# Turning q, k and v in two parts, with the loads behind the store, in a decoder layer on one core

## The chip, the cores and the metric

The kernel runs on one core of a Trainium2 chip. Its time is the device time of one execution in microseconds, the median of the runs shown. A core has TensorE (PE, matrix products, with its weight loads shown apart as PEld), VectorE (DVE), ScalarE (ACT), GpSimd (POOL) and SyncE (SP); here SP and POOL issue nearly all DMA transfers. SBUF is the memory on the chip that all operands pass through, PSUM holds the results of PE.

## The reference

One layer of a decoder on 512 new tokens and, beside them, on 8 single tokens with a state of their own (520 columns in all):

```python
xn = rmsnorm(h, norm_mix)
proj = xn @ w_in                         # q | k | v | z | beta, decay logits | pool channels
qkv_c, new_conv = short_conv(conv_buf, qkv, conv_w)      # 4 taps along time, then silu
q = l2norm(q) * 128 ** -0.5;  k = l2norm(k)
o, S = gated_delta_chunked(q, k, v, g, beta, S0)         # 8 heads of 128, chunks
dn_out = rmsnorm(o, dn_norm) * silu(z)
pool_out = multiscale_pool(p) ...
h = h + concatenate([dn_out, pool_out]) @ w_out
gu = rmsnorm(h, norm_ffn) @ w_gate_up
h = h + (silu(gu[:, :5632]) * gu[:, 5632:]) @ w_down

# gated_delta_chunked, per head and chunk
kb = k * beta
m = strict_lower((kb @ k.T) * decay)
u = triangular_solve(I + m, v * beta)
w = triangular_solve(I + m, kb * exp(g))
qk = lower((q @ k.T) * decay)
v_new = u - w @ S                        # chunk after chunk
o = (q * exp(g)) @ S + qk @ v_new
S = S * exp(g_last) + (k * exp(g_last - g)).T @ v_new
```

The model has a width of 2048; the state of the 512 tokens starts at zero, and so do the three rows ahead of the convolution (its left edge).

## The kernel before

**Products.** All data are fp32, cut into a high and a low part; each product of a tile of 128 weight columns is three matmuls (high·high, high·low, low·high, L168 to L170) for each of 16 blocks of the depth and for each of two chunks of columns (264 and 256). That is 96 matmuls, written out by `product()`, the second chunk three blocks behind the first. The results go to three PSUM banks (`mm`), from which DVE evicts them (`normed_out`, L259). Weights come as `raw` by SP (L131), ACT makes `hi` (L135), DVE makes `lo` (L137).

**What is woven in.** PE executes in the order in which the program writes its instructions. Between the products, `product()` calls `weave.step()` once per block of depth, six matmuls. A `Weave` holds tracks of generators: at each step, the first generator of each track goes on to its next `yield`, and the number that it yields is the number of steps to its next turn; `add(task, track, delay)` puts a task at the end of a track, to start no sooner than `delay` steps from now. A step is thus a distance on PE. The other engines have their instructions ordered by the framework's scheduler, by priority and by when operands are there, and each engine and each DMA queue works its list in order.

**The mixer.** For two batches `b` of four heads `h` (0 to 3, then 4 to 7) the program runs:
- four key tiles: product, convolution over 3 + 512 columns in a tile `ext` whose left three columns are zero (`columns()`, L263; the taps at L739), silu (L740), a turn of the blocks, and 16 steps later `keys(h)`, which makes the Gram matrix of k, its sums of squares (L799 to L808), the masked matrix of each chunk into `mixb` (L810) and stores its diagonal blocks of 32 (`nd_d`, L816);
- `eliminate(b)`: loads the blocks of four heads (`nb`, L825), clears `u` (L829), inverts all blocks in 62 steps on DVE (L835, L837), copies the transpose (`ut`, L840), and stores both (`ud_d`, L838, L841);
- four z tiles (called z0 to z3 below for b = 0);
- for each head `qv_tiles(h)`: loads the inverted blocks (`utf`, L1117), the v tile, the q tile, and then `delta(h)`. The products for v and q of this head stand on PE around the delta of the head before.

`delta(h)` begins with `decay(h)` (broadcast `gcb` by SP, four subtractions on DVE to `dm`, L779, an exponential on ACT, L781), the exponential of `gcb` (L851) and q's scaling `qts` (L853). Then comes what is called the solution here: four matmuls `nn`·`utf` to `xp` (L859), their copy `xt_` on ACT (L861), a copy of `utf` to `cur` on POOL (L863), and three times (`it`) four matmuls of `xt_` (L869) with the combination of their result on DVE (L871), at a distance of two steps. After the last, q·k and its decay (`aq`, L881). The decay of the keys (`kd`, L874) and the scaling of v (L754) are put on DVE between them. Then four chunks in turn, with the state `S` (L909) handed on.

**A turn.** k, q, v and the result are needed with time along the partitions too. `turn_blocks` does this with one transpose of 32 x 32 blocks on DVE (L766, L763), a store to memory (`tok_d`, L768) and four loads back (L771), all five transfers issued by POOL one after the other. Each load waits on POOL's queue for the store to be through.

Of the kernel before, what the change touches and what calls it, by code (L numbers as in the profile page):

```python
# [8 lines left out]
F32 = mybir.dt.float32  # L9
# [3 lines left out]
ALU = mybir.AluOpType  # L13
# [29 lines left out]
class Weave:  # L43
# [3 lines left out]
    def __init__(self):  # L47
        self.tracks, self.wait, self.now = ([], []), [0, 0], 0
# [21 lines left out]
def decoder_kernel(ctx, tc, x_prompt, x_sample, state_delta, state_conv, state_pool, norm_mix, w_in,  # L70
# [189 lines left out]

    def columns():
        ext = pre.tile([P, 3 + SEQ], F32, tag="ext", name="ext", bufs=2)
        pool.memset(ext[:, 0:3], 0.0)  # L263
        return ext
# [256 lines left out]
    with ExitStack() as p1:  # L521
# [235 lines left out]
        def turn_blocks(kind, h, src, dst):  # L757
# [7 lines left out]
            else:  # L765
# [3 lines left out]
                rows = d.rearrange("(i p) (j f) -> j p i f", p=32, j=4)  # L769
            for j in range(4):  # L770
                pool.dma_start(dst[32 * j:32 * j + 32, :].rearrange("p (n q) -> p n q", n=rows.shape[2]), rows[j])  # L771

# [17 lines left out]
        def keys(h):  # L790
# [26 lines left out]
            for q in range(4):  # L817
                r = slice(32 * q, 32 * q + 32)
                pool.memset(nn3[r, :, r], 0.0)


        def eliminate(b):
# [5 lines left out]
            yield 10  # L828
# [16 lines left out]
        def delta(h, qT, qk, vs):  # L845
# [6 lines left out]
            qts = d1tile("qts", [P, SEQ], "qts")  # L852
            dve.tensor_tensor(qts, qT, gcb, op=ALU.mult)  # L853
# [11 lines left out]
            for it in range(3):  # L865
# [9 lines left out]
                if it == 2:  # L875
# [4 lines left out]
                    for c in range(NCH):  # L880
                        dve.scalar_tensor_tensor(aq[:, ck(c)], gq_[:, ck(c)], fk[:, c:c + 1], dm[:, ck(c)],  # L881
                                                 op0=ALU.mult, op1=ALU.mult)
                if it == 1:
                    scaled(vs, ik)
# [4 lines left out]
            for c in range(NCH):  # L889
# [26 lines left out]
                if c == 1:  # L916
                    ss = d1tile("ss", [P, NCH], "ss")
                    junk = d1tile("junk", [P, P], "junk")
                    for j in range(NCH):
                        act.activation(by_column(junk), by_chunk(qk)[:, j], AF.Square, accum_out=ss[:, j:j + 1])  # L920
# [16 lines left out]
            turn_blocks(3, h, on, on)  # L937
            weave.add(gate(h, on), 1, 12)
# [174 lines left out]
        def qv_tiles(h):  # L1113
# [6 lines left out]
            turn_blocks(2, h, vs, vs)  # L1120
            qT = d1tile("s0", [P, SEQ], "qT")
            qkv_tile(0, h, qT)
            qk = d1tile("tq", [P, SEQ], "qk")
            turn_blocks(0, h, qT, qk)
            weave.add(delta(h, qT, qk, vs), 0, 1)

        kds = {}
        for b in range(2):
            for h in range(4 * b, 4 * b + 4):
# [5 lines left out]
                kds[h] = d1tile("kd", [P, SEQ], "kd")  # L1135
                turn_blocks(1, h, mixb[:, h % 4, 0:SEQ], kds[h])
# [23 lines left out]
        for t in (6, 7, 4, 5, 2, 3, 0, 1):  # L1160
            pool_tile(t, operands)
            if t % 2:
                weave.add(pool_mix(t // 2, *splits[t // 2]), 1, 12 if t > 1 else 7)
# [942 lines left out]
```

## Time and profile before

| | |
|---|---|
| median of 3 runs | 2160.54 us (2160.06 to 2163.25) |
| profiled execution | 2161.12 us |
| its span | 2159.4 us |
| PE, PEld busy | 2127.0 us (98%), 2118.4 us (98%) |
| DVE, ACT, POOL busy | 1772.2 us (82%), 919.9 us (43%), 531.4 us (25%) |
| mean granted clock of PE | 0.998 |
| moved by DMA | 313.84 MB, 145 GB/s on the mean |

The span is the time from the first to the last instruction on the core; 1.7 us of the execution lie around it. Busy times of one engine do not add to those of another, since the engines work side by side. A row of the timeline shows start, duration, engine, line, operation, output and inputs, shape, and in brackets the idle time of that engine just before it and what ended it. A row of the waits shows the engine, its output and line, the engine, tile and line that it waited for, and then the sum of the waits, their number and the longest.

### The profile page before, as it was taken

The page shows a single profiled execution, that of the slowest core. Times are in us where ns is not written, and L with a number is a line of the kernel's source. Part 1 is how long each engine was busy: PE and PEld are TensorE (multiplying, and loading weights), DVE is VectorE, ACT ScalarE, POOL GpSimd, SP SyncE. Part 2 cuts the span into 40 slices and gives each one's busy share as a digit, 9 for nine tenths or more (in the row PEclk, how much of TensorE's full clock was granted, in tenths as well). Part 3 has the DMA queues.
Part 4 walks back from the last instruction along what each step waited for, and adds up shares of the span by engine and source line. Part 5 has one row for each costly group of instructions (what it writes and reads, how often), then busy time and mean ns, then how long its engine had stood idle before and what let it go on. Part 6 is the DMA issues. An engine that isn't in the chain of part 4 may idle for free.

```text
span 2159.4 us, 43083 instructions
## 1 busy us (share of the span) xinstructions
PE 2127.0 (98%) x17681; PEld 2118.4 (98%) x17681; DVE 1772.2 (82%) x2715; ACT 919.9 (43%) x1340; POOL 531.4 (25%) x672
## 2 busy tenths in 40 slices
PE   8999999999999999999999999999999999999998
PEld 7999999999999999999999999999999999999998
DVE  7886677667599979988988988988877898887997
ACT  6433433343264544434434434434334444435444
POOL 2413441332012202233233233232113302003100
PEclk9999999999999999999999999999999999999999
DMA  8444454544445533554554454454456746438333
GB/s 281 126 125 118 130 141 122 132 125 126 122 118 162 156 114 115 150 167 141 144 164 144 143 168 142 142 169 133 121 147 189 233 112 205 115 104 248 91 108 119
DMA packets 449154, 313.84 MB, mean 145 GB/s; under 512 B 29116, under 2 KB 425813, under 8 KB 445613
## 3 DMA queue, kind: packets, MB, share of 16 engines
q1 hardware_dynamic: 422733, 219.94, 36.5%
q0 software_dynamic: 24912, 90.34, 13.4%
q8 instruction: 139, 2.28, 0.5%
q10 hardware_dynamic: 1312, 0.80, 0.1%
q14 instruction: 58, 0.48, 0.1%
HBM read 259.86 MB, written 51.82 MB: 144 GB/s over the span
## 4 chain that ended last, share of the span: by engine, by line
PE 82%; DVE 9%; DMA 3%; issue 2%; ACT 2%; POOL 1%; SPq 0%; DVEq 0%; ACTq 0%; POOLq 0%
PE dn L1252 21%; PE dn L1251 21%; PE dn L1253 21%; PE mm L168 5%; PE mm L169 5%; PE mm L170 5%; DVE lo L1245 1%; DMA vs<-tok_d 1%; DVE lo L137 1%; DVE y L739 1%; DMA st<-a_d 1%; DVE raw L1273 1%; PE dn L869 1%; DMA tok_d<-bt 1%; ACT hi L1244 0%
## 5 line engine op out<-in xcount | busy, mean ns | idle before, releaser
L1245 DVE TENSOR_TENSOR lo<-raw,hi 128x1024 fp32r<-128x1024 f32 (+1 forms) x422 | 527.9, 1271 | 89.0 <-ACT hi L1244 86.8
L1244 ACT CAST hi<-raw 128x1024 fp32r<-128x1024 f32 (+1 forms) x422 | 427.8, 1027 | 401.2 <-DVE raw L1273 195.5
L168 PE MATMUL mm<-xh,hi 128*128 128x256 f32 (+1 forms) x1280 | 380.3, 297 | 1.8 <-DVE mixa L259 1.8
L169 PE MATMUL mm<-xl,hi 128*128 128x256 f32 (+1 forms) x1280 | 362.1, 283 | 0.9 <-DVE xl L350 0.5
L170 PE MATMUL mm<-xh,lo 128*128 128x256 f32 (+1 forms) x1280 | 362.2, 283 | 0.4 <-DVE lo L137 0.4
L168 PEld LDWEIGHTS mm<-xh,hi 128*128 128x128 f32 x1280 | 242.1, 189 | 3.0 <-DVE mixa L259 2.2
L169 PEld LDWEIGHTS mm<-xl,hi 128*128 128x128 f32 x1280 | 242.3, 189 | 1.7 <-DVE xl L350 1.7
L170 PEld LDWEIGHTS mm<-xh,lo 128*128 128x128 f32 x1280 | 241.3, 189 | 0.6 <-DVE lo L137 0.6
L1252 PE MATMUL dn<-b21l,hi 128*128 128x260 f32 x620 | 175.8, 284 | 0.3 <-DVE b21l L1815 0.3
L1253 PE MATMUL dn<-b21h,lo 128*128 128x260 f32 x620 | 175.4, 283 | 0.0
L1251 PE MATMUL dn<-b21h,hi 128*128 128x260 f32 x620 | 175.0, 282 | 0.0
L1253 PE MATMUL dn<-b11h,lo 128*128 128x260 f32 x612 | 173.2, 283 | 1.3 <-DVE lo L1245 1.3
L1273 DVE TENSOR_TENSOR raw<-raw 128x1024 f32<-128x1024 f32 (+1 forms) x130 | 172.0, 1323 | 2.2
L1437 POOL TENSOR_TENSOR mixa<-mixa 128x520 f32<-128x520 f32 x22 | 50.2, 2280 | 501.6 <-DVE mixa L1431 501.6
L1252 PE MATMUL dn<-b11l,hi 128*128 128x260 f32 x612 | 173.3, 283 | 0.0
L1251 PE MATMUL dn<-b11h,hi 128*128 128x260 f32 x612 | 172.7, 282 | 0.0
L1251 PE MATMUL dn<-T1h,hi 128*128 128x260 f32 x556 | 158.1, 284 | 0.0
L1252 PE MATMUL dn<-T1l,hi 128*128 128x260 f32 x556 | 157.7, 284 | 0.0
L1253 PE MATMUL dn<-T1h,lo 128*128 128x260 f32 x556 | 156.7, 282 | 0.0
L1251 PE MATMUL dn<-B22h,hi 128*128 128x260 f32 x548 | 155.9, 284 | 0.0
L1252 PE MATMUL dn<-B22l,hi 128*128 128x260 f32 x548 | 155.6, 284 | 0.0
L1253 PE MATMUL dn<-B22h,lo 128*128 128x260 f32 x548 | 154.6, 282 | 0.4 <-DVE lo L1245 0.4
(664 smaller groups left out, 6552.6 us busy)
## 6 DMA issues: line engine op xcount, KB each, us to landing
raw<-in_w_gate_up_dram SPq DMA_DIRECT2D x134, 512.0 KB
raw<-in_w_in_dram SPq DMA_DIRECT2D x79, 512.0 KB
a_d<-mixa POOLq DMA_DIRECT2D x22, 1040.0 KB, 5.5
raw<-in_w_down_dram SPq DMA_DIRECT2D x48, 448.0 KB
mixb<-in_w_gate_up_dram SPq DMA_DIRECT2D x41, 512.0 KB
raw<-in_w_out_dram SPq DMA_DIRECT2D x25, 512.0 KB
st<-a_d POOLq DMA_DIRECT2D x49, 260.0 KB, 6.4
raw<-in_w_down_dram SPq DMA_DIRECT2D x24, 512.0 KB
```

The lines of the kernel that those rows point to most:

```text
L137: dve.tensor_tensor(lo[:, r], raw[:, r], hi[:, r].bitcast(F32), op=ALU.subtract)
L168: te.matmul(acc[ci], wh, hi[k][:, c0:c1], start=(k == 0), stop=False)
L169: te.matmul(acc[ci], wh, lo[k][:, c0:c1], start=False, stop=False)
L170: te.matmul(acc[ci], wl, hi[k][:, c0:c1], start=False, stop=(k == len(w) - 1))
L739: dve.scalar_tensor_tensor(y, ext[:, i:i + SEQ], cw(i, t), y, op0=ALU.mult, op1=ALU.add)
L1244: act.copy(hi, raw)
L1245: dve.tensor_tensor(lo, raw, hi.bitcast(F32), op=ALU.subtract)
L1251: te.matmul(acc, wh[:, k, :], xf[:, k, :], start=start and k == 0, stop=False)
L1252: te.matmul(acc, wh[:, k, :], xg[:, k, :], start=False, stop=False)
L1253: te.matmul(acc, wl[:, k, :], xf[:, k, :], start=False, stop=stop and k == wh.shape[1] - 1)
L1273: dve.tensor_tensor(r[name], r[a], r[b], op=op)
L1437: pool.tensor_tensor(q[:, 4:8:2, :], q[:, 1:4:2, :], q[:, 0:2, :], op=ALU.subtract)
```

## The change

- `turn_blocks` becomes a generator `turn`: the transpose and the store, then six steps later the four loads. All turns run on a track of their own (2), those of k five steps after their tile, of v five, of q nine (17 for the first head of a batch), of the result three after the delta. The gate follows the loads of the result on a further track (3).
- q's scaling is written behind the solution and not ahead of it.
- The two tiles `ext` are allocated once and their left edge is zeroed once.
- The clearing of the stored blocks in `mixb` (`cleared`) becomes a task five steps behind the stores; `eliminate` yields 14 steps in place of 10 after issuing `nb`; the `delta` of heads 0 and 4 starts 12 steps after its q tile in place of 1; q's sums of squares come one chunk later; `pool_mix` of the first pair of pool tiles starts 20 steps behind and not 12.

```diff
-        self.tracks, self.wait, self.now = ([], []), [0, 0], 0
+        self.tracks, self.wait, self.now = ([], [], [], []), [0] * 4, 0
...
+    exts = [pre.tile([P, 3 + SEQ], F32, tag="ext", name="ext", bufs=2) for _ in range(2)]
+    for ext in exts:
+        pool.memset(ext[:, 0:3], 0.0)
+
     def columns():
-        ext = pre.tile([P, 3 + SEQ], F32, tag="ext", name="ext", bufs=2)
-        pool.memset(ext[:, 0:3], 0.0)
-        return ext
+        exts.append(exts.pop(0))
+        return exts[1]
...
-        def turn_blocks(kind, h, src, dst):
+        def turn(kind, h, src, dst):
...
+            yield 6
+            if kind == 0:
+                dst = qks[h] = d1tile("tq", [P, SEQ], "qk")
             for j in range(4):
                 pool.dma_start(dst[32 * j:32 * j + 32, :].rearrange("p (n q) -> p n q", n=rows.shape[2]), rows[j])
+            if kind == 3:
+                weave.add(gate(h, dst), 3, 8)
+
+        def query_rows(h, qT):
+            yield from turn(0, h, qT, None)
+
+        def key_rows(h):
+            kds[h] = d1tile("kd", [P, SEQ], "kd")
+            yield from turn(1, h, mixb[:, h % 4, 0:SEQ], kds[h])
+
+        def cleared(h):
+            nn3 = v3(mixb[:, 4 + h % 4, 0:SEQ])
+            for q in range(4):
+                r = slice(32 * q, 32 * q + 32)
+                pool.memset(nn3[r, :, r], 0.0)
+            yield 1
...
-            for q in range(4):
-                r = slice(32 * q, 32 * q + 32)
-                pool.memset(nn3[r, :, r], 0.0)
+            weave.add(cleared(h), 2, 5)
...
-            yield 10
+            yield 14
...
             act.activation(gcb, gcb, AF.Exp)
-            qts = d1tile("qts", [P, SEQ], "qts")
-            dve.tensor_tensor(qts, qT, gcb, op=ALU.mult)
...
                                                  op0=ALU.mult, op1=ALU.mult)
+                    qts = d1tile("qts", [P, SEQ], "qts")
+                    dve.tensor_tensor(qts, qT, gcb, op=ALU.mult)
                 if it == 1:
                     scaled(vs, ik)
...
-                if c == 1:
+                if c == 2:
...
-            turn_blocks(3, h, on, on)
-            weave.add(gate(h, on), 1, 12)
+            weave.add(turn(3, h, on, on), 2, 3)
...
-            turn_blocks(2, h, vs, vs)
+            weave.add(turn(2, h, vs, vs), 2, 5)
...
-            turn_blocks(0, h, qT, qk)
-            weave.add(delta(h, qT, qk, vs), 0, 1)
+            weave.add(query_rows(h, qT), 2, 9 if h % 4 else 17)
+            weave.add(delta(h, qT, vs), 0, 1 if h % 4 else 12)
...
-                turn_blocks(1, h, mixb[:, h % 4, 0:SEQ], kds[h])
+                weave.add(key_rows(h), 2, 5)
...
-                weave.add(pool_mix(t // 2, *splits[t // 2]), 1, 12 if t > 1 else 7)
+                weave.add(pool_mix(t // 2, *splits[t // 2]), 1, 20 if t == 7 else 12 if t > 1 else 7)
```

How the order of instructions moves is shown at three places. In the new order the lines have other numbers: L859, L861, L869 are now L877, L879, L887; L781 and L851 are L803 and L871; L799, L801, L810 are L821, L823, L832; L779, L874 are L801, L892; L835 and L837 are L855 and L857.

The first is PE at the first `delta` (head 0), where `mm` are the product's PSUM banks, `utf0` the inverted blocks and `xt_` the copy. Before:

```order
L170 MATMUL mm_2125<-xh_96,lo_2114 128x256
L859 MATMUL dn_2152<-utf0_645,mixb_99 128x96 x4
L168 MATMUL mm_2124<-xh_96,hi_2113 128x264
L169 MATMUL mm_2124<-xl_97,hi_2113 128x264
L170 MATMUL mm_2124<-xh_96,lo_2114 128x264
L168 MATMUL mm_2125<-xh_96,hi_2113 128x256
```

And now:

```order
L170 MATMUL mm_2107<-xh_96,lo_2102 128x256
L877 MATMUL dn_2198<-utf0_645,mixb_99 128x96 x4
L168 MATMUL mm_2106<-xh_96,hi_2101 128x264
L169 MATMUL mm_2106<-xl_97,hi_2101 128x264
L170 MATMUL mm_2106<-xh_96,lo_2102 128x264
L168 MATMUL mm_2107<-xh_96,hi_2101 128x256
L169 MATMUL mm_2107<-xl_97,hi_2101 128x256
L170 MATMUL mm_2107<-xh_96,lo_2102 128x256
L168 MATMUL mm_2107<-xh_96,hi_2101 128x256
L169 MATMUL mm_2107<-xl_97,hi_2101 128x256
L170 MATMUL mm_2107<-xh_96,lo_2102 128x256
L887 MATMUL dn_2218<-utf0_645,xt__2203 96x96 x4
```

The solution's first matmuls stood near the start of the product, with twelve product matmuls between L859 and the first L869; now they stand at its end, 66 rows further on in PE's list, with nine between L877 and the first L887.

The second is ACT at the same place, from q's activation on (`qT`), with a weight cast (`hi`), the exponentials (`dm`, `gcb`) and the copy `xt_`. Before:

```order
L740 ACTIVATE qT<-y 128x512
L861 COPY xt__2157<-dn 128x384
L781 ACT_TABLE_LOAD
L781 ACTIVATE dm<-dm 128x512
L851 ACTIVATE gcb<-gcb 128x512
L135 CAST hi<-raw 128x1024
```

And now:

```order
L743 ACTIVATE qT<-y 128x512
L135 CAST hi<-raw 128x1024
L803 ACT_TABLE_LOAD
L803 ACTIVATE dm<-dm 128x512
L871 ACTIVATE gcb<-gcb 128x512
L879 COPY xt__2203<-dn 128x384
```

The copy has moved behind the cast, the table load and the two exponentials.

The third is DVE between the keys of head 3 and the start of the elimination (`tm`, `u`), where L259 evicts the products' first (128x264) and second chunks. Before:

```order
L810 SCALAR_TENSOR_TENSOR mixb<-dn,sck,dm 128x128 x4
L137 TENSOR_TENSOR lo<-raw,hi 128x1024
L779 SCALAR_TENSOR_TENSOR dm<-gcb,gcs,mneg 128x128 x4
L874 TENSOR_TENSOR kd<-kd,sck 128x512
L137 TENSOR_TENSOR lo<-raw,hi 128x1024
L259 TENSOR_TENSOR mixa<-mm,rb 128x264
L835 TENSOR_TENSOR tm<-nb,u 64x31
L837 TENSOR_TENSOR u<-u,tm 64x31
L835 TENSOR_TENSOR tm<-nb,u 64x60
L259 TENSOR_TENSOR mixa<-mm,rb 128x256
```

And now:

```order
L892 TENSOR_TENSOR kd<-kd,sck 128x512
L259 TENSOR_TENSOR mixa<-mm,rb 128x264
L832 SCALAR_TENSOR_TENSOR mixb<-dn,sck,dm 128x128 x3
L259 TENSOR_TENSOR mixa<-mm,rb 128x256
L832 SCALAR_TENSOR_TENSOR mixb<-dn,sck,dm 128x128
L801 SCALAR_TENSOR_TENSOR dm<-gcb,gcs,mneg 128x128 x4
L137 TENSOR_TENSOR lo<-raw,hi 128x1024 x2
L855 TENSOR_TENSOR tm<-nb,u 64x31
L857 TENSOR_TENSOR u<-u,tm 64x31
L855 TENSOR_TENSOR tm<-nb,u 64x60
L857 TENSOR_TENSOR u<-u,tm 64x30x2
```

The eviction of z1 now stands behind the second `kd` scaling and the small scales, and that of z2, which stood ahead of the elimination, now comes behind its third pair (three rows after the last one shown). The scaling `qts` keeps its place relative to the combinations on DVE, and on SP the weight load that stood between the `nd_d` stores of head 3 now stands ahead of all four.

More of the change, by code (lines that the diff above doesn't have):

```diff
@@ L842, in eliminate, with delta @@
             yield 1
-        def delta(h, qT, qk, vs):
+        def delta(h, qT, vs):
             kT, nn, kd = mixb[:, h % 4, 0:SEQ], mixb[:, 4 + h % 4, 0:SEQ], kds[h]
@@ L919, in delta @@
                     for j in range(NCH):
-                        act.activation(by_column(junk), by_chunk(qk)[:, j], AF.Square, accum_out=ss[:, j:j + 1])
+                        act.activation(by_column(junk), by_chunk(qks[h])[:, j], AF.Square, accum_out=ss[:, j:j + 1])
                     dve.tensor_scalar(ss, ss, EPS, None, op0=ALU.add)
@@ L1119, in qv_tiles @@
             qkv_tile(2, h, vs)
-            turn_blocks(2, h, vs, vs)
+            weave.add(turn(2, h, vs, vs), 2, 5)
             qT = d1tile("s0", [P, SEQ], "qT")
             qkv_tile(0, h, qT)
-            qk = d1tile("tq", [P, SEQ], "qk")
-            turn_blocks(0, h, qT, qk)
-            weave.add(delta(h, qT, qk, vs), 0, 1)
-        kds = {}
+            weave.add(query_rows(h, qT), 2, 9 if h % 4 else 17)
+            weave.add(delta(h, qT, vs), 0, 1 if h % 4 else 12)
+        kds, qks = {}, {}
         for b in range(2):
@@ L1134, in decoder_kernel @@
                     weave.add(gates(), 1)
-                kds[h] = d1tile("kd", [P, SEQ], "kd")
-                turn_blocks(1, h, mixb[:, h % 4, 0:SEQ], kds[h])
+                weave.add(key_rows(h), 2, 5)
                 weave.add(keys(h), 1, 16)
```

## The prediction

> **What bounds the kernel now.** I read the page's totals first, then the chain of waits of PE, then stretches of the timeline around the few waits that lie where the change works.
>
> ```profile
> span 2159.4 us, 43083 instructions
> PE 2127.0 (98%) x17681; PEld 2118.4 (98%) x17681; DVE 1772.2 (82%) x2715; ACT 919.9 (43%) x1340; POOL 531.4 (25%) x672
> PE dn L859 <- DMA utf<-ud_d: 4.5, 1, 4.5
> PE dn L869 <- DVE uu L871: 3.1, 6, 0.6
> PE mm L168 <- DVE mixa L259: 1.8, 1, 1.8
> PE dn L894 <- DVE S L909: 1.6, 1, 1.6
> L1245 DVE TENSOR_TENSOR lo<-raw,hi 128x1024 fp32r<-128x1024 f32 (+1 forms) x422 | 527.9, 1271 | 89.0 <-ACT hi L1244 86.8
> ```
>
> PE works through 98% of the span, and the change removes no matmul. So the only thing to be had is PE's idle time, 2159.4 − 2127.0 = 32.4 us at most, and of that only what the mixer's part holds: the four waits (total, count, longest one), 11.0 us together. The other idle time on PE lies in the load of the inputs and in the feed-forward, which the diff doesn't touch. POOL is busy for a quarter of the span. Its long waits for the turns (`kd`, `qk`, `mixb`) hold up nothing that PE waits for, so the split of the turns is worth something only through what it lets move elsewhere. All terms below are therefore waits of PE. (The last row gives the price of a subtraction of 128x1024 on DVE, which L137 does too: 1.27 us.)
>
> **The change, part by part.**
>
> *1. The first solution 11 steps later: −4.5.* The longest wait is that of the first `delta`, whose first matmul (L859) needs the elimination's result, read back as `utf`:
>
> ```profile
> 158.27 0.28 PE L170 MATMUL mm<-xh,lo 128*128 128x264 f32 x1
> 158.98 0.28 PE L170 MATMUL mm<-xh,lo 128*128 128x256 f32 x1
> 163.80 1.57 PE L859 MATMUL dn<-utf,mixb 128*128 128x96 f32 x6 [4.53 <-DMA utf<-ud_d]
> 155.25 0.61 SPq L838 DMA_DIRECT2D ud_d<-u  x1
> 159.63 1.32 SPq L1117 DMA_DIRECT2D utf<-ud_d  x3
> ```
>
> The six matmuls from 158.27 to 158.98 take 0.71 us, 0.12 each. In the new order 66 more product matmuls stand ahead of L859 on PE (the 11 additional steps of its delay), so PE gets there 66 × 0.12 = 7.9 us later than 163.80 − 4.53 = 159.3, at about 167.2. `utf` landed at 163.8 and does not come later, since the elimination keeps its place on DVE though it yields 14 and not 10. The wait goes whole, with 3.4 us to spare. The second half of the heads has no such wait; the same shift there is worth nothing, and its matmuls are only in another order.
>
> *2. The half clock behind that wait: −2.5.*
>
> ```profile
> 155.80:162.60 6.80, 3.46 (x30) 3.26 (x28) 4.70 (x8) 1.05 (x1) 3.36 (x7) 1.00 0.91 241
> 162.60:169.40 6.80, 5.60 (x28) 5.63 (x29) 5.20 (x9) 2.78 (x4) 1.28 (x3) 0.50 0.55 140
> 169.40:176.20 6.80, 6.80 (x64) 6.80 (x63) 2.39 (x7) 1.44 (x3) 2.79 (x5) 1.00 0.27 56
> ```
>
> (Busy time and count of PE, weight loads, DVE, ACT and POOL, then the granted clock.) In the 6.8 us after the wait the clock stands at 0.50 and PE gets through 28 matmuls in 5.6 us; in the next stretch it does 64 in 6.8, which for 28 is 3.0. At the 0.12 of above it would be 3.3. So the wait costs another 2.3 to 2.6 us, and without it this goes too: I take 2.5. The Trainium skill, "TensorE: Matmul & The Clock Gate", section "What's actually happening", describes this: an idle window of some 3.4 us halves the clock until a busy one has passed. The trace agrees (a wait of 4.53 us, a granted clock of 0.50 behind it), and by the page's rule the loss would be half of the 5.6 us, 2.8. The sum does not use it.
>
> *3. The wait of z3 for its PSUM bank: −1.6.* The first matmul of the last z tile waits until DVE has evicted an earlier one (L259):
>
> ```profile
> 135.41 0.39 PE L168 MATMUL mm<-xh,hi 128*128 128x256 f32 x1 [1.79 <-DVE mixa L259]
> 134.94 0.42 DVE L259 TENSOR_TENSOR mixa<-mm,rb 128x264 f32<-128x264 f32 x1
> 123.59 0.20 DVE L835 TENSOR_TENSOR tm<-nb,u 64x31 f32<-64x31 f32 x1 [3.88 <-DMA nb<-nd_d]
> 134.60 0.41 DVE L837 TENSOR_TENSOR u<-u,tm 64x247 f32<-64x247 f32 x1
> 113.58 1.26 SPq L816 DMA_DIRECT2D nd_d<-mixb  x3
> 114.94 0.39 SPq L131 DMA_DIRECT2D raw<-in_w_in_dram  x1
> 115.37 2.04 SPq L816 DMA_DIRECT2D nd_d<-mixb  x1
> 119.89 0.54 SPq L825 DMA_DIRECT2D nb<-nd_d  x1
> ```
>
> This eviction stands in DVE's order inside the elimination, 134.94 + 0.42 − 123.59 = 11.8 us after its start. Now two more pairs of multiplication and subtraction (2 × 0.41 each) and one more L259 (0.42) stand between, 2.1 us, so it ends 13.9 us after that start. But the start itself comes sooner: it waits for `nb`, which landed 123.59 − 119.89 = 3.7 us after its issue, and that issue stood behind the fourth `nd_d` store, which was held until 117.4 behind a weight load. In the new order that load stands ahead of all four stores; four stores at 1.26/3 = 0.42 from 113.6 on end at 115.3. `nb` was issued 119.89 − 117.41 = 2.5 after the last store, with one broadcast and one weight load between as now, so it goes at 117.8 and lands at 121.5. The bounds are 120.9 (the load between needn't wait for its buffer) and 123.6 (as before). Then the eviction is done at 121.5 + 13.9 = 135.4, and PE, which asked for the bank at 135.41 − 1.79 = 133.6 and now asks 1.5 later (term 5), at 135.1, loses 0.2 to 0.3 instead of 1.8.
>
> *4. q's scaling behind the solution: −1.5.* Six matmuls L869 wait for DVE (L871), 0.5 to 0.6 us each, since between two L871 stand other operations:
>
> ```profile
> 201.95 0.54 DVE L871 SCALAR_TENSOR_TENSOR uu<-dn,utf 96x384 f32<-96x384 f32 x1
> 202.73 0.71 DVE L766 STREAM_TRANSPOSE bt<-qT 128x512 f32<-128x512 f32 x1 [0.23 <-ACT qT L740]
> 203.37 0.65 DVE L853 TENSOR_TENSOR qts<-qT,gcb 128x512 f32<-128x512 f32 x1
> 203.94 0.41 DVE L871 SCALAR_TENSOR_TENSOR uu<-dn,utf 96x256 f32<-96x256 f32 x1
> ```
>
> That is 0.71 + 0.65 = 1.36 us of other work. In the new DVE order the scaling, though written later, keeps this place (the scheduler puts it where its operands are ready); only the transpose moves, and not for every head: two heads now have one L137 there (1.27), two keep the 1.36, two have the scaling alone (0.65). With 0.65 the waits vanish, with the rest they stay. Bounds 0 and −3.1; I take half, −1.5.
>
> *5. A new wait at z1: +1.5.* The eviction of the first chunk of the last key tile stands further back on DVE:
>
> ```profile
> 108.08 0.69 DVE L874 TENSOR_TENSOR kd<-kd,sck 128x512 f32<-128x512 f32 x1
> 108.69 0.28 DVE L799 SCALAR_TENSOR_TENSOR junk<-dn,ident 128x128 f32<-128x128 f32 x1
> 108.90 0.43 DVE L259 TENSOR_TENSOR mixa<-mm,rb 128x264 f32<-128x264 f32 x1
> 112.42 1.12 DVE L810 SCALAR_TENSOR_TENSOR mixb<-dn,sck,dm 128x128 f32<-128x128 f32 x4
> ```
>
> It ended at 109.33. Two more L799, two more `kd` scalings and five small operations on `ss` and `sck` now come first, 2 × 0.28 + 2 × 0.69 + about 0.6 (five of the smallest kind, by the 0.20 of the small row of term 3 less its overlap), which is 2.5, so it ends near 111.9. PE asks for that bank two products ahead of 133.6, each 96 matmuls of 0.12 or 11.5 us, at 110.6. The difference is 1.3. Bounds 0 (the work ahead of it is fed sooner) and 3 (the L137 between waits too); I take 1.5, near the difference.
>
> *6. The same at z2: +0.3.* Its eviction stood ahead of the elimination and now stands behind its first three pairs:
>
> ```profile
> 119.27 0.43 DVE L259 TENSOR_TENSOR mixa<-mm,rb 128x264 f32<-128x264 f32 x1 [0.16 <-PE mm L170]
> ```
>
> Three pairs (six operations of a little over 0.20, 1.3) and the eviction (0.43) end at 121.5 + 1.7 = 123.2; PE asks at 133.6 − 11.5 + 1.5 = 123.6. That is no wait, by 0.4. With `nb` as late as before it is 123.6 + 1.7 = 125.3, a wait of 1.7, and 3.2 with term 5 at zero; below nothing it cannot go, as there was no wait. I take 0.3.
>
> *7. The copy for the first solution behind other work on ACT: +1.8.*
>
> ```profile
> 163.01 0.69 DVE L754 TENSOR_TENSOR vs<-vs,sck 128x512 f32<-128x512 f32 x1 [2.48 <-DMA vs<-tok_d]
> 157.43 1.05 ACT L135 CAST hi<-raw 128x1024 fp32r<-128x1024 f32 x1 [3.08 <-issue]
> 165.83 0.48 ACT L861 COPY xt__2157<-dn 128x384 f32<-128x384 f32 x1
> 166.32 1.28 ACT L781 ACT_TABLE_LOAD   x1
> 169.01 0.63 ACT L781 ACTIVATE dm<-dm 128x512 f32<-128x512 f32 x1 [1.41 <-DVE dm L779]
> 169.55 0.62 ACT L851 ACTIVATE gcb<-gcb 128x512 f32<-128x512 f32 x1
> ```
>
> The first L869 needs the copy L861 of what L859 made. Before, it stood right behind q's activation; now a weight cast, the table load and two exponentials stand between. The first exponential waits for DVE until 169.0, and DVE's part there starts with `vs`, whose turn is no earlier (its transpose now stands behind the copy of the elimination's result, which comes some 2.1 us earlier): the copy ends at about 169.2 + 0.63 + 0.62 + 0.48 = 170.9. PE gets to the first L869 behind L859 (1.57 at half the clock, 0.8 at the full) and nine matmuls (1.1), at 167.2 + 1.9 = 169.1. The difference is 1.8. Bounds 0 and 4 (L779 held further by a late `vs`).
>
> *The rest: 0.* The 17 small memsets removed on POOL, the memsets of `cleared`, the later squares on ACT and the eight stores and loads of the turns that change place on POOL's queue have as cover POOL's 75% of idle time; if that is gone, the first thing late is `vs`, which is the slower rival. The wait for `S` (1.6) stays. On SP the third group of `utf` loads waits some 5 us longer, with weight loads behind it that are about 20 us ahead of their use.
>
> Sum: 2161.12 (the profiled execution) − 4.5 − 2.5 − 1.6 − 1.5 + 1.5 + 0.3 + 1.8 = 2154.6. The median before is 2160.54, 0.6 below that execution, so 2154.0.
>
> **Rivals.** What tells a change from none here is about 0.2%, 4.3 us.
>
> *The gain of the first wait is eaten.* `nb` lands as late as before, since the weight load ahead of it waits for its buffer: z2 then waits 1.7 in place of 0.3, and z3 (137.5 against 135.1 + 1.7) 0.7 in place of 0.2, in all 1.9 worse: 2155.9. With terms 5 and 7 at their upper ends as well it is 2155.9 + 1.5 + 2.2 = 2159.6. For it speaks that a store already waited 2.04 us there behind a weight load, and that three of my terms are waits that the trace of before doesn't have; against it that the four stores now stand ahead of the load that waits. It is the way to no measurable change. By the rule of the Trainium skill cited in term 2, a new wait of over 3.4 us would cost a stretch of half clock besides, 2.5 by the rows of that term; only term 7's upper end comes near it, and 2162 would be the time.
>
> *The `vs` loads get late: slower.* POOL holds them now behind the clearing of the next elimination's buffer:
>
> ```profile
> 157.35 2.18 POOL L771 DMA_DIRECT2D vs<-tok_d  x4 [2.29 <-issue]
> 159.52 0.97 POOL L829 MEMSET u<- 64x1024 f32 x1
> ```
>
> Before, the loads went ahead of it. That memset waits until `u` has been stored. If the loads landed after about 163.3, each further us would move L754, L779 and the copy of term 7 by as much, and PE with them. To be slower by 4.3 it would take 10.8 us more than my forecast: 8.3 of waiting, with loads that land near 171.6, and 2.5 of half clock behind it, about 2165. Against it: the store of `u` at 155.25, some 2.1 earlier now, is through 4.4 us later at most (the `utf` loads, which need it, go at 159.63), so at 157.5; with 0.97 for the memset the loads go at 158.5 instead of 157.35, about 1 us late.
>
> *More than I think.* No new wait at z1 or on ACT, and all L869 waits gone: 2154.0 − 1.5 (z1) − 0.3 − 1.8 (ACT) − 1.6 (the other half of term 4) = 2148.8.
>
> **How the numbers follow.** My own case (a gain of 4.3 to 9): 0.48. More: 0.20. Eaten: 0.24. Slower: 0.08. Terms 1 and 2 are the surest, since they rest on one wait and the distance it moves; all others are below 2 us each, and of the eaten case a little (0.01) still gains over 4.3 and of my own a little does not. So faster 0.68, the same 0.24, slower 0.08. The range goes from the larger gain, 2148.5, to the eaten case with its bounds, 2159.6, rounded to 2160.0; about 1 in 10 is left out on either side.
>
> **What would show it.** Right: L859 no longer in the list of PE's waits, no stretch with a granted clock of 0.50 near 165, L168's wait for L259 below 0.5 at z3 and a new one of 1 to 2 at z1 near 112; `nb` landed near 121.5; the first L869 waiting for ACT's L861 (now L879) by 1 to 2; three or so waits of L869 for `uu` left. Wrong: PE waiting over 3 us anywhere before 200 us, above all for the copy or for `vs`; a second half of the heads (near 340 to 420 us) with waits that were not there; `utf` landing after 167; or a difference in the feed-forward, where I expect none.

## The result, and the profile after

The change made the kernel slower by a little: 2165.4 us (median of ten, 2163.89 to 2170.53) against 2161.1 us, a ratio of 1.0023 with a 95% interval of 1.0013 to 1.0032. The trace shows the fastest of the ten executions, so it holds 2.8 of the 4.3 us. Its totals and the longest waits of PE (total, count, longest):

```profile
span 2162.2 us, 43048 instructions
PE 2126.3 (98%) x17681; PEld 2116.5 (98%) x17681; DVE 1768.0 (82%) x2715; ACT 923.1 (43%) x1342; POOL 533.4 (25%) x650
PE dn L887 <- DVE uu L889: 6.3, 6, 1.5
PE mm L168 <- DVE mixa L259: 4.1, 2, 2.7
PE dn L887 <- ACT xt__2203 L879: 1.9, 1, 1.9
PE dn L921 <- DVE R L916: 1.3, 2, 0.7
PE dn L914 <- DVE S L929: 0.9, 1, 0.9
```

The wait for `utf` is gone, as forecast. In its place the waits of the solution for `uu` have doubled (3.1 to 6.3), those for an evicted bank (L259) have grown from 1.8 to 4.1, and the copy `xt_` and `R` are waited for. Three of these waits stand in the timeline at z1, z2 and the first solution:

```profile
111.74 0.38 PE L168 MATMUL mm<-xh,hi 128*128 128x256 f32 x1 [1.33 <-DVE mixa L259]
126.25 0.58 PE L168 MATMUL mm<-xh,hi 128*128 128x256 f32 x1 [2.73 <-DVE mixa L259]
174.65 0.58 PE L887 MATMUL dn<-utf,xt__2203 128*96 128x96 f32 x4 [1.86 <-ACT xt__2203 L879]
```

Behind the wait at z2 PE ran at half the clock for 3.4 us (stretches of the same trace; PE's busy time and matmuls come first, the granted clock stands third from the end):

```profile
122.80:126.22 3.42, 0.72 (x7) 0.52 (x5) 1.67 (x8) 0.00 (x0) 0.00 (x0) 1.00 0.23 57
126.22:129.63 3.41, 3.38 (x15) 3.38 (x16) 3.13 (x11) 1.78 (x3) 0.00 (x0) 0.50 0.00 0
```

The whole stretch in which the two programs differ, in one row each of the same view: first before, then after, then a second trace of the changed kernel.

```profile
100.00:640.00 540.00, 528.60 (x4453) 526.00 (x4452) 390.73 (x920) 206.64 (x387) 142.24 (x266) 0.99 0.47 126
```

```profile
100.00:640.00 540.00, 524.81 (x4420) 521.22 (x4419) 386.05 (x910) 205.44 (x383) 139.36 (x246) 1.00 0.47 125
```

```profile
100.00:640.00 540.00, 525.09 (x4411) 521.67 (x4410) 385.19 (x906) 205.35 (x382) 138.90 (x246) 0.99 0.47 125
```

PE idles 540 − 528.6 = 11.4 us before and 15.2 after. In this stretch half clock lasted 6.8 us before and 3.4 after, and it costs about half of that. Idle time plus half of the half clock is 14.8 before, 16.9 after and 18.3 in the second trace (14.9 idle, 6.8 of half clock): the spans are 2159.4, 2162.2 and 2162.8. The span less this sum is 2144.6, 2145.3 and 2144.5 in these three, and 2141.8 to 2146.7 over all 20 traces, so the sum accounts for the spans within some 2.5 us.

### The profile page after: what moved, and what is told of

Same layout as the page of the kernel before. It is cut to its first block, busy times and chain, and to the rows that moved or that the text cites. A ratio compares the mean times of both kernels' runs of the same rounds, so it can differ in the third digit from the quotient of the medians.

```text
span 2162.2 us, 43048 instructions
## 1 busy us (share of the span) xinstructions
PE 2126.3 (98%) x17681; PEld 2116.5 (98%) x17681; DVE 1768.0 (82%) x2715; ACT 923.1 (43%) x1342; POOL 533.4 (25%) x650
## 4 chain that ended last, share of the span: by engine, by line
PE 82%; DVE 8%; DMA 4%; issue 2%; ACT 2%; POOL 1%; SPq 0%; DVEq 0%; ACTq 0%; POOLq 0%
PE dn L1269 21%; PE dn L1268 21%; PE dn L1270 21%; PE mm L168 5%; PE mm L170 4%; PE mm L169 4%; DVE lo L1262 1%; DMA vs<-tok_d 1%; DVE lo L137 1%; DMA st<-a_d 1%; DMA gcb<-gcr_d 1%; DVE y L742 1%; DVE raw L1290 0%; DMA tok_d<-bt 0%; DVE u L857 0%
## 5 line engine op out<-in xcount | busy, mean ns | idle before, releaser
L1268 PE MATMUL dn<-b11h,hi 128*128 128x260 f32 x612 | 172.8, 282 | 0.0
L1270 PE MATMUL dn<-T1h,lo 128*128 128x260 f32 x556 | 156.8, 282 | 0.0
```

What stands on the lines that cost most here:

```text
L1268: te.matmul(acc, wh[:, k, :], xf[:, k, :], start=start and k == 0, stop=False)
L1270: te.matmul(acc, wl[:, k, :], xf[:, k, :], start=False, stop=stop and k == wh.shape[1] - 1)
```

## The experiments

Each was timed against the kernel before on the same chip. "Before" is at 2160.0 to 2161.1 in all of them. b_ kernels are the kernel before with one part, a_ kernels the changed one with one part taken back or altered.

**The changed kernel once more.**

> The changed kernel once more, unchanged, for a second trace. The first trace was that of its fastest execution (2163.89, the median of ten was 2165.4) and shows one stretch of half clock, 3.4 us. If executions differ by how many waits tip a stretch of 3.4 us below half busy: the same waits on PE within 0.3 us each, and a time that differs from 2163.9 by about 1.7 us for each further stretch of half clock (2165.6 with two, 2167.3 with three). Rival: the waits themselves differ from execution to execution by more than 1 us.

2165.0 us, ratio 1.0023 (1.0011 to 1.0035). Both answers were half right. The two long waits in PE's timeline:

```profile
112.35 0.39 PE L168 MATMUL mm<-xh,hi 128*128 128x256 f32 x1 [1.82 <-DVE mixa L259]
174.56 0.47 PE L887 MATMUL dn<-utf,xt__2203 128*96 128x96 f32 x1 [3.70 <-ACT xt__2203 L879]
```

And the stretch that holds the first of them, with the next:

```profile
109.50:112.92 3.42, 1.60 (x13) 1.39 (x12) 3.35 (x11) 2.06 (x3) 0.21 (x2) 1.00 0.59 148
112.92:116.33 3.41, 3.41 (x18) 3.41 (x17) 3.01 (x8) 3.14 (x5) 0.59 (x3) 0.50 0.37 90
```

Half clock followed z1's wait here, and the wait at z2 is missing, for two reasons: PE, slowed, came to it 2.0 us later (125.5 against 123.5), and `nb` landed 1.5 us sooner (122.9 against 124.4, see below), so that the eviction was done at 124.7. Time was then lost at the copy (3.70 against 1.86). The waits in the heads behind are the same within 0.3 us. So a wait does not keep its place: what PE loses early, it need not wait for later.

**k's turn, alone and taken back.**

```diff
-                turn_blocks(1, h, mixb[:, h % 4, 0:SEQ], kds[h])
+                weave.add(key_rows(h), 2, 5)
```

a_keysnow is the changed kernel with only this undone, b_keys2 the kernel before with only this done.

> The changed kernel with k's turn alone as before: store and loads right behind the key tile, not five and six steps later. Theory 1 (the waits at z1 and z2 come from VectorE's order, which k's later turn shifts): the order at the key tiles and at the elimination's start is again that of before, so the waits of 1.4 and 2.7 us and the half clock at z2 (1.7 or more) go, and the one at z3 (1.8) comes back: about -4, 2161.5 against 2165.4; the waits for uu stay near 6. Theory 2 (they come from something else, such as the clearing task or nb's load): no change within 1 us.

> The kernel before with one part of the change alone: k's turn in two parts (store five steps behind the key tile, loads six steps later). Theory 1 (k's later turn alone makes VectorE's order at z1 and z2): the waits at z1 (about 1.4) and z2 (about 2.7) appear, with or without a half clock behind, the one at z3 (1.8) goes. As the first delta is not delayed here, the wait for utf takes most of it up: it falls from 4.5 to 1.5 to 2.5 and its half clock goes, so the time stays within 2 us of before, 2159 to 2162. Theory 2 (these waits need another part of the change): none of the three waits moves.

Taken back (a_keysnow): 2160.6 us, ratio 0.9999 (0.9990 to 1.0008): all of the loss, 4.3 us, is gone. Alone on the kernel before (b_keys2): 2167.5 us, 1.0034 (1.0021 to 1.0046), which is more than the whole change loses. The longest waits of a_keysnow in the mixer:

```profile
PE dn L887 <- DVE uu L889: 6.0, 6, 1.6
PE mm L168 <- DVE mixa L259: 2.0, 2, 1.4
PE dn L887 <- ACT xt__2203 L879: 1.3, 1, 1.3
```

The evictions of the first chunk at z1 and z2 on DVE, in the changed kernel and then in a_keysnow:

```profile
111.26 0.42 DVE L259 TENSOR_TENSOR mixa<-mm,rb 128x264 f32<-128x264 f32 x1
125.78 0.42 DVE L259 TENSOR_TENSOR mixa<-mm,rb 128x264 f32<-128x264 f32 x1
108.78 0.42 DVE L259 TENSOR_TENSOR mixa<-mm,rb 128x264 f32<-128x264 f32 x1
119.42 0.43 DVE L259 TENSOR_TENSOR mixa<-mm,rb 128x264 f32<-128x264 f32 x1 [0.98 <-PE mm L170]
```

The stretch at z1 in b_keys2, and the one behind it:

```profile
109.94:113.36 3.42, 1.64 (x14) 1.44 (x14) 3.34 (x12) 2.44 (x4) 0.40 (x2) 1.00 0.62 163
113.36:116.77 3.41, 3.41 (x18) 3.41 (x17) 2.40 (x6) 3.38 (x5) 0.79 (x4) 0.50 0.43 106
```

Theory 1 holds for the cause: k's turn moves `kd` and the small scales of the next keys ahead of z1's eviction on DVE, and the start of the elimination ahead of z2's. In a_keysnow the waits at z1 and z2 are gone, the old one at z3 (1.4) is back, and no stretch between 100 and 640 us has half clock. In b_keys2 the wait at z1 came (1.8) and the one at z3 went, as theory 1 said, but none came at z2. The seven traces with k's later turn fall into two groups: four wait 0.9 to 1.4 at z1 and then 2.3 to 2.7 at z2, and three wait 1.8 to 2.2 at z1, run at half clock right behind it, and do not wait at z2. The expectation for b_keys2 failed in its time: the wait at the first delta fell to 1.9, as I had it, but its half clock stayed, the first solution then waited 2.3 for `uu`, a z tile of the second half waited 1.8, and four stretches of half clock (13.6 us, 6.8 of cost) came where before had 6.8 us (3.4).

**The delay of the first delta.**

```diff
-            weave.add(delta(h, qT, qk, vs), 0, 1)
+            weave.add(delta(h, qT, qk, vs), 0, 1 if h % 4 else 12)   # b_delay12
+            weave.add(delta(h, qT, qk, vs), 0, 1 if h else 7)        # b_delay7_h0
-            weave.add(delta(h, qT, vs), 0, 1 if h % 4 else 12)
+            weave.add(delta(h, qT, vs), 0, 1)                        # a_delay1
+            weave.add(delta(h, qT, vs), 0, 1 if h else 12)           # a_delay12_h0
```

> The kernel before with one part of the change alone: the delta of heads 0 and 4 starts 12 steps after its q tile and not 1. Theory 1 (the later deltas push the end of one head's result on VectorE into the next head's solution): the 4.5 us wait for utf and the half clock behind it go (-7), the six waits of the solution for uu grow from 3.1 to about 6, the copy of the first solution costs about 2; net -2 to -4, so 2157 to 2159 us against 2161.1. Theory 2 (the growth of these waits comes from the turns in two parts): they stay near 3.1, net -5 to -7, 2154 to 2156.

> The changed kernel with the delta of heads 0 and 4 back at 1 step (and q's turn of these heads at 9 steps, as for the others). Theory 1: the waits for uu fall from 6.3 to about 3.1, the waits for R (1.3) and for the copy (1.9) go, a wait for utf of 2 to 4 us comes back, perhaps with a half clock of 2.5: 2160 to 2165. Theory 2: the waits for uu stay above 5, with utf on top 2166 to 2169. The waits at z1 (1.4) and z2 (2.7) stay in both.

> The changed kernel with the 12 steps for head 0 alone; head 4 starts after 1 step (its q turn after 9). Theory 1: the three waits for uu in the second half (1.25, 1.8, 0.6) fall to about 0.55 each and one wait for R (0.7) goes: about -2.5, 2163 against 2165.4. Theory 2: all stay, no change.

> The kernel before with the delta of head 0 alone starting 7 steps after its q tile: the most that leaves the delta of head 1 at its place on PE (36 matmuls later for head 0, none for the others). Theory 1 (what cost in the 12 steps is that the next heads' deltas move too): the wait for utf falls from 4.5 to below 0.5 and the half clock of 6.8 us behind it goes, against at most 2 us of new waits (the copy, the result's scaling in head 1's solution): -4 to -7, 2154 to 2156.5 against 2160.5. Rival (any shift of head 0's delta is paid back by waits behind it): within 2 us of before.

b_delay12: 2166.2 us, 1.0023 (1.0014 to 1.0031). a_delay1: 2167.1, 1.0032 (1.0022 to 1.0043). a_delay12_h0: 2168.2, 1.0032 (1.0021 to 1.0044). b_delay7_h0: 2160.7, 0.9998 (0.9989 to 1.0007). Waits of b_delay12:

```profile
PE dn L869 <- DVE uu L871: 6.8, 5, 2.2
PE dn L901 <- DVE R L896: 2.3, 3, 1.2
PE dn L869 <- ACT xt__2223 L861: 2.0, 1, 2.0
```

And of a_delay1:

```profile
PE dn L887 <- DVE uu L889: 7.3, 7, 4.1
PE dn L926 <- ACT W L923: 3.1, 2, 2.8
PE dn L877 <- DMA utf<-ud_d: 1.7, 1, 1.7
```

On the mechanism theory 1 was right for b_delay12 and the two a_ kernels. With the delay alone the waits for `uu` rise to 6.8; without it, they are back at 0.5 to 0.6 for the six later heads (7.3 − 4.1 = 3.2 in all), and in a_delay12_h0 for those of the second half. The reason stands in the changed kernel's DVE list at the solution of head 2:

```profile
233.92 0.68 DVE L956 TENSOR_TENSOR mixb<-dn,ro 128x512 f32<-128x512 f32 x1
234.52 0.74 DVE L742 SCALAR_TENSOR_TENSOR y<-ext,prm,y 128x512 f32<-128x512 f32 x1
235.18 0.55 DVE L889 SCALAR_TENSOR_TENSOR uu<-dn,utf 96x384 f32<-96x384 f32 x1
235.64 0.69 DVE L764 STREAM_TRANSPOSE bt<-mixb 128x512 f32<-128x512 f32 x1
236.27 0.64 DVE L902 TENSOR_TENSOR qts<-qT,gcb 128x512 f32<-128x512 f32 x1
```

L956 and L764 are the result of head 1, whose delta now stands 30 matmuls later: its scaling comes ahead of head 2's first `uu` and its transpose behind it, where before both were done 6 to 7 us earlier. What counts is the distance between two deltas, and not whether the later one moves: in b_delay7_h0 head 1's delta keeps its place on PE and head 0's comes 36 matmuls nearer, and head 1 waits 1.75 for its first `uu`, with the scaling and the transpose of head 0's result (L936 at 200.2, L761 at 201.5) ahead of it.

On the times, theory 1 missed all four, and b_delay7_h0 came out as its rival had it, within 2 us of before. I had counted the wait for `utf` as a gain to be kept, and each kernel gave it back elsewhere. In b_delay7_h0 it fell from 4.5 to 1.0, but head 0 waits 2.0 for `uu`, head 1 the 1.75, and half clock lasts 6.8 us as before. In a_delay1 it is `uu` of head 0 (4.1) and `W` at head 4 (2.8; ScalarE is held there by q's squares, which waited 5.8 us for q's loads); in a_delay12_h0 the wait for `W` at head 4 is 3.8. The 12 steps in the second half, which remove no wait of before, thus seem to cover q's later turn; a_k4 below, with 4 steps, has no wait for `W`, but one of 2.3 for `S` there.

**The same delay in smaller doses,** with k's turn as before.

```diff
-            weave.add(query_rows(h, qT), 2, 9 if h % 4 else 17)
-            weave.add(delta(h, qT, vs), 0, 1 if h % 4 else 12)
+            weave.add(query_rows(h, qT), 2, 9 if h % 4 else n + 5)   # n = 4, 7, 9, 10
+            weave.add(delta(h, qT, vs), 0, 1 if h % 4 else n)
```

> As the kernel with 7 steps, but with 4 (q's turn at 9): if the delay is a trade between the wait for utf and the waits behind it, utf is waited for by about 2 us, q's squares hold the copy W on ScalarE by 1 to 2 us at heads 0 and 4, and the time is 1 to 3 us above that with 7 steps, 2157 to 2160.

> The changed kernel with k's turn as before, and heads 0 and 4 delayed by 7 steps instead of 12 (q's turn of these heads by 12 and not 17), so that the deltas of heads 1 and 5 keep their places on PE. Theory 1 (the growth of the waits for uu from 3.1 to 6, and those for R and S of 931, come from these deltas being moved): the waits for uu of heads 1, 2, 3 and 5, 6, 7 fall back to 0.5 to 0.6 each and those for R go; utf is waited for by 1 us or less, without a half clock: 2155 to 2158 against 2160.6 for the same with 12 steps. Rival (they come from the turns in two parts): uu stays near 6, 2160 to 2162.

> As the kernel with k's turn as before and 7 steps of delay, but with 9 (the deltas of heads 1 and 5 move by 2 steps instead of 0 at 7 and 5 at 12). Theory 1 (the delay is a trade: too short and head 0's solution waits for vs and S, 2.0 and up to 1.9 us; too long and the next heads' solutions wait for uu, over 1 us each): every single wait stays under 1.7 us, no half clock, the sum of the waits between 100 and 620 us falls by 2 to 4 against 12 steps: 2157 to 2159. Rival (the waits only change places, whatever the delay): 2160 to 2163, as with 7 and 12.

> The same with 10 steps (deltas of heads 1 and 5 moved by 3). Theory 1: 2157.5 to 2159.5, near that with 9. Rival: 2160 to 2163.

With 4, 7, 9, 10 and 12 steps: 2169.1, 2163.2, 2168.7, 2165.5 and 2160.6 us; ratios 1.0037 (1.0023 to 1.0051), 1.0011 (1.0002 to 1.0020), 1.0037 (1.0025 to 1.0050), 1.0020 (1.0011 to 1.0029) and that of a_keysnow. There is no best value between 7 and 12: the trade theory fell. The longest waits in the mixer of a_k7:

```profile
PE dn L887 <- DVE uu L889: 5.1, 7, 2.0
PE dn L914 <- DVE S L929: 4.0, 3, 1.9
```

And of a_k9:

```profile
PE dn L914 <- DVE S L929: 4.7, 3, 2.8
PE dn L887 <- DVE uu L889: 4.6, 6, 1.0
PE dn L926 <- ACT W L923: 3.1, 2, 2.1
```

With 7 steps the deltas of heads 1 and 5 stay, and their waits for `uu` are 0.5 again, as theory 1 said; but head 0 waits 2.0 for `uu` and head 4 waits 1.9 for `S`. With 4 steps these deltas stay too, yet heads 1 and 5 wait 2.0 and 1.9. The waits change places. a_k7 also shows how far executions of one kernel differ: the traced one, 2159.7 us, has no half clock between 100 and 640 us, and its eleven executions go from 2159.6 to 2166.2, the three slowest at a mean granted clock of 0.997, the others at 0.999 to 1.000. The clock is a part of this, but not shown to be all: those others differ by 4.4 us among themselves. a_keysnow, whose waits between 100 and 640 us are all at 1.6 or below, goes from 2159.7 to 2161.4.

**nb's landing.**

```diff
-            sp.dma_start(nb...)         # a_nbact: act.dma_start(nb...)
+            with tc.high_priority(offset=2 * AHEAD):    # b_hp: here and at the stores nd_d
+                sp.dma_start(nb...)
```

> The changed kernel with nb (the read of the eliminate's blocks) issued on ScalarE's DMA queue in place of SyncE's, where it stood behind a weight load. Theory A (nb landed 8 us after its issue because it queued behind that load): it lands within 4 us, near 120.5, the wait at z2 (2.7) and the half clock behind it go: -4 to -6, about 2160. Theory B (the 16 DMA engines themselves are full then, whatever the queue): nb lands within 1 us of 124.4, no change in time.

> The kernel before with the four stores of the blocks of each head and nb's load given a higher priority, so that no weight load stands between the stores of head 3 on SyncE's queue. Theory A (nb's landing is set by its issue): it is issued near 117.5 and lands near 121.5 instead of 123.6, the wait for utf falls by about 2: 2157 to 2158.5. Theory B (the DMA engines are full with the weight and broadcast loads around it, as in the changed kernel, where it landed 8 us after its issue): it lands at 123 to 124.5, no change in time.

a_nbact: 2166.8 us, 1.0027 (1.0018 to 1.0037). b_hp: 2163.0, 1.0014 (1.0006 to 1.0023). The rows of the changed kernel's timeline for SyncE's queue and DVE:

```profile
113.08 1.74 SPq L838 DMA_DIRECT2D nd_d<-mixb  x4
115.84 0.40 SPq L131 DMA_DIRECT2D raw<-in_w_in_dram  x1
116.42 0.53 SPq L845 DMA_DIRECT2D nb<-nd_d  x1
119.65 0.39 SPq L131 DMA_DIRECT2D raw<-in_w_in_dram  x1
124.38 0.20 DVE L855 TENSOR_TENSOR tm<-nb,u 64x31 f32<-64x31 f32 x1 [4.75 <-DMA nb<-nd_d]
```

And those of a_nbact, where ScalarE's queue issues it:

```profile
116.28 0.50 ACTq L845 DMA_DIRECT2D nb<-nd_d  x1
124.42 0.20 DVE L855 TENSOR_TENSOR tm<-nb,u 64x31 f32<-64x31 f32 x1 [4.54 <-DMA nb<-nd_d]
```

In the second trace of the changed kernel (a_again) the next weight load came later:

```profile
117.02 0.53 SPq L845 DMA_DIRECT2D nb<-nd_d  x1
121.79 0.39 SPq L131 DMA_DIRECT2D raw<-in_w_in_dram  x1
122.91 0.20 DVE L855 TENSOR_TENSOR tm<-nb,u 64x31 f32<-64x31 f32 x1 [1.14 <-DMA nb<-nd_d]
```

In the changed kernel `nb` was issued even earlier than forecast (116.4 against 117.8), and landed 8.0 us later, not 3.7. On ScalarE's queue it landed at the same moment: theory B, the DMA engines are taken by the weight loads around it (their busy share is 0.9 or more in each microsecond from 118 to 123). The time to landing follows those loads. It is 3.7 before and 3.5 in a_keysnow, where the weight load ahead was issued 5.0 and 5.6 us earlier; 4.8 in b_hp, with the load ahead 2.4 us earlier. Where that load was issued 0.2 to 0.6 us ahead, as in all seven traces with k's later turn, it is 5.4 to 5.9 in the three whose next load follows after 4.7 us or more, and 7.6 to 8.1 in the four whose next load follows after 3.2 to 3.6. The four are those that wait at z2. In b_hp, issued at 117.5, it landed at 122.3, between the theories; yet the wait for `utf` stayed at 4.5, and half clock behind it lasted 13.7 us. So an earlier start of the elimination by 1.3 us did not bring PE forward.

**Smaller parts.**

```diff
-            turn_blocks(2, h, vs, vs)          # a_vnow: v's turn again at once
+            weave.add(turn(2, h, vs, vs), 2, 5)
-            dve.tensor_copy(ut, ...)
+            act.copy(ut, ...)                  # b_utact, a_k9_utact
# b_small: qts behind the solution, ext tiles zeroed once, squares at c == 2
```

> The changed kernel with v's turn alone as before. Theory 1 (vs landed at 167 instead of 163 because its store and loads stand later on GpSimd's queue, behind the clearing of u): vs lands near 163, the copy xt_ ends some 4 us earlier and the wait for it (1.9) goes: -1.5 to -2.5, about 2163.5; the waits for uu stay near 6, as they come from the delay. Rival: the waits for uu fall too (they come from v's late loads): -4 to -5, 2161.

> The kernel before with three small parts of the change: q's scaling written behind the solution, the ext tiles with their left edge zeroed once, q's squares at the third chunk. Theory 1 (these do next to nothing, as VectorE's order keeps the scaling's place): within 1.5 us of before, 2159 to 2162, and six waits for uu of 0.5 us as before. Rival (the scaling off the solution's way shortens them): the waits for uu fall below 1.5 in all, -2.

> The kernel before with the copy of the elimination's result (L840, 1.12 us on VectorE) made by ScalarE instead. It tests whether the stretch from nb to utf is bound by VectorE's list: if so, v's transpose behind it comes 1.1 us earlier and utf is no later: the wait for utf stays near 4.5, -0.5 to -1.5 in all. If utf waits for this copy alone, as ScalarE starts it later behind a weight cast, utf lands up to 1 us later: +1.

> The kernel with k's turn as before and 9 steps, with the same copy on ScalarE. vs lands about 1 us sooner, head 0's solution waits about 1 us less: 0 to -1.5 against the kernel with 9 steps.

b_small: 2160.2 us, 1.0000 (0.9991 to 1.0008), six waits for `uu` of 3.1 in all: q's scaling written later does nothing. a_vnow: 2166.6, 1.0034 (1.0022 to 1.0047); both theories missed the time, `vs` still landed at 166.6 (transposed at 155.2, behind the elimination's copy) and the wait at z1 was 2.2. b_utact: 2162.6, 1.0008 (0.9999 to 1.0016), unclear; the copy takes 2.13 us on ScalarE, and the wait for `utf` is 5.4, nearer to the second answer. a_k9_utact: 2172.0, 1.0050 (1.0037 to 1.0062); this expectation failed, as `vs` landed 1.1 us later than in a_k9 (163.9 against 162.8) and not sooner, and the wait for `xt_` grew from 2.6 to 3.8.

**A product in front instead of a delta behind.**

```diff
-            for h in range(4 * b, 4 * b + 4):
+            for h in ((0, 1, 2, 3, 4), (5, 6, 7))[b]:
                 z_tile(h)
```

> The kernel before with the z tile of head 4 moved from the second to the first half of the heads (five z tiles, then three), and nothing else. It gives the elimination's result one product (11.5 us) more time in the first half without moving any delta against its own head's tiles, which is what the 12 steps do. If the gain of the change was lost by moving the deltas against their neighbours' tiles: the wait for utf (4.5) and its half clock (3.4 at most) go, no new waits in the solutions (six of 0.5), and the second half, where utf landed some 9 us ahead of its use, waits for it 1 to 2.5 us at most: 2154 to 2157.5 against 2160.5. If VectorE's list in this stretch has no room at all, whatever the order on PE: the waits come back elsewhere, within 2 us of before.

2162.6 us, 1.0011 (1.0002 to 1.0020). In the first half it did as hoped: no wait for `utf`, none for `xt_`, `uu` at 0.7 or less per head (3.2 in all). But the second half then waits for `utf`, in the timeline of PE:

```profile
394.75 0.50 PE L859 MATMUL dn<-utf,mixb 128*128 128x96 f32 x1 [8.69 <-DMA utf<-ud_d]
```

The stretches around it, with the granted clock third from the end:

```profile
386.33:389.74 3.41, 0.00 (x0) 0.00 (x0) 1.36 (x2) 0.00 (x0) 0.74 (x1) 1.00 1.02 218
389.74:399.98 10.24, 5.23 (x25) 5.26 (x26) 5.20 (x9) 3.44 (x5) 3.06 (x7) 0.50 0.60 113
```

It runs 10.2 us at half clock besides. PE reached this wait at 394.75 − 8.69 = 386.1, where before it stood at 390.3 at the same instruction: 4.2 us ahead, in spite of 3.4 us of half clock at z3. The expectation had allowed 1 to 2.5 us here. The last `utf` load was issued 10.8 us later than before (392.7 against 381.9) and PE came 4.2 sooner, 15.0 in all for a wait of 8.7, so there were some 6 us of room before and not the 9 that I had counted on. The wait for `utf` can therefore be had for nothing in one half, by room in front, and not by moving a delta against its neighbours; this kernel has no spare product for the other half. No version tried beats the kernel before clear of the noise.

## Why the prediction was wrong, step by step

- **Terms 1 and 2, right where they stood.** The wait for `utf` and the half clock behind it went (−4.5, −2.5 to −3.4).
- **Term 3, right in size, wrong in reason.** z3's wait went, but because PE came late from z2 (139.4, with the eviction done at 138.2) and not because `nb` was early. That the size fits is luck.
- **Term 5, right:** 1.33 and 1.82 measured, 1.5 forecast. **Term 7, right** in the first trace (1.86 against 1.8) and near its upper end in the second (3.70). Both its ends came 3.7 us later than I had them, the copy at 174.6 and PE at 172.8, since `vs` landed at 167.1 and PE had lost time at z1 and z2. In a_keysnow, without those losses, they are 170.6 and 169.3, against 170.9 and 169.1 forecast.
- **Term 6, wrong: +0.3 forecast, 2.73 measured, and 1.7 of half clock behind it.** The step that failed is "issued at 117.8, landed 3.7 later": it was issued at 116.4 and landed 8.0 later, at 124.4 and not at 121.5, and the eviction behind it ended at 126.2 and not at 123.2. I carried the time to landing over from before, where the weight load ahead had mostly landed (the busy share of the DMA engines falls to 0.11 from 120 to 121). The rival "eaten" had the late landing, though for another reason (a load that waits for its buffer); I gave its wait 1.7 and the half clock only from 3.4 us on. a_keysnow shows the cause, the order that k's turn makes: 1.33 and 2.73 and 1.7 of half clock, less the 1.4 that come back at z3, are 4.4, and the kernel without that part is 4.3 nearer to before. That the two agree so well is in part luck, since the spans of the two traces differ by 2.5 only.
- **Term 4, wrong in sign: −1.5 forecast, +3.2 measured.** I misread the rows: the waits are not for the second combination, between which and the first the transpose and q's scaling stand, but for the first, behind the taps of the convolution. Before, at head 1:

```profile
199.72 2.32 DVE L739 SCALAR_TENSOR_TENSOR y<-ext,prm,y 128x512 f32<-128x512 f32 x3
202.64 0.52 PE L869 MATMUL dn<-uu,xt__2555 128*96 128x64 f32 x4 [0.50 <-DVE uu L871]
```

The first combination ended at 202.49, the second started only at 203.94; all six waits of before are of this kind. So there was nothing to gain from q's scaling, which b_small confirms, and I didn't look at what arrives from the head before. "The same shift there is worth nothing" was the failed sentence: the 30 matmuls by which the deltas of heads 1 and 5 move bring their results into the next solution. The delay runs show it; the 1.3 for `R`, which no term had, appears with it. Head 3's wait grows as well (0.6 to 1.2) though its delta and head 2's keep their places; no run shows why.
- **The sum itself.** In the first trace the terms come to −4.5 − 3.4 − 1.8 + 3.2 + 1.3 + 2.7 + 1.7 + 1.9, and 1.3 for `R` and −0.2 for `S` besides: +2.2, where the spans differ by 2.8. So terms 4 and 6, with its half clock, hold 8.8 us of the error, and `R` another 1.3. The terms were added as if independent. They are not: b_keys2 and a_again show that a loss at z1 changes what is lost at z2, at `utf` and at the copy, and k's turn alone and the delay alone each cost more (7.4 and 5.8 us) than the whole change. The rival "slower" named 2165, but with `vs` landing near 171.6; it landed at 167.1, so the agreement is luck.
- **The clock.** The forecast kept half clock for long waits. By the Trainium skill, "TensorE: Matmul & The Clock Gate", section "What's actually happening", an idle window of about 3.4 us halves the clock, and the window runs freely. The traces agree with the free grid of 3.41 us and not with "idle": a window with PE busy for 1.60 of 3.42 us was enough (a_again above).

What stays open: why `vs` takes some 10 to 12 us from its transpose to its landing (153.4 to 163.0 before, 156.8 to 167.1 and 155.4 to 167.0 in the two traces of the changed kernel), so late that the first solution depends on it, and why 12 steps with k's turn as before are better than 9 or 10.

## What to carry to other kernels

When work woven between products is moved, follow the tail of the task as well as its head: where its last operations fall on a shared in-order engine, and which neighbour's chain they meet. A wait that is taken away on a chain with little slack returns at the next thing that is late; before counting it, look how far ahead the next operands are. And count the time of a transfer from what else is in flight, not from its own issue.

## What the runs showed of the hardware

The clock's state changes on a grid of 3.413 us that starts at a different point of the program in each execution. Over the 20 traces I took each such window between 60 and 2100 us at full clock with PE under 0.6 busy: after all 28 windows that were busy for 0.467 or less came one at half clock, after all 5 from 0.53 to 0.6 one at full clock, and between these it went either way (7 of 16 at half). At half clock, all 10 windows busy for 0.81 or less were followed by another at half; of 38 at 0.93 or more, 35 were followed by full clock. So a single wait of 1.8 us can cost another 1.7, if it falls within one window and not across two. This fits that a_k7, with several waits near 2 us, scatters by 6.5 us, and a_keysnow, with none above 1.6, by less than 2. It is not shown to be the whole of the scatter: the fastest and the slowest execution of the changed kernel (2163.89 and 2170.53 us) have the same mean granted clock, 0.998.
